# Four blocks of an output projection with another matmul stream: every second element, even then odd, backwards, and alternating PSUM banks

## Chip, cores and metric

The kernel runs on one core of one Trainium2 chip. The metric is the device time of one execution in microseconds (us); lower is better.

## What is computed

One decoder layer on 256 tokens of width 4096: a combined input projection, three head groups that run side by side (windowed attention with sinks and a relative bias, an mLSTM, cross-attention into 256 memory tokens), a SiLU gate on each, then one output projection and a LayerNorm over the scaled residual. The part that the change touches is the output projection:

```python
mix = jnp.concatenate([a_out, m_out, c_out], axis=-1).astype(x.dtype)
y = jnp.einsum("bse,ed->bsd", mix, w_out)
x = layer_norm(DEEPNORM_ALPHA * x.astype(jnp.float32) + y.astype(jnp.float32),
               ln_g, ln_b).astype(x.dtype)
```

Here `mix` is 256 x 4096 and `w_out` 4096 x 4096, all fp32.

## The kernel before, in words

Every large product keeps fp32 accuracy by splitting each operand into a rounded part and a rest, both of type fp32r: `split` (L91 to L93) makes `hi` with a cast on ScalarE (ACT) and `lo = raw - hi` on VectorE (DVE). A product is then three matmuls, hi by hi, hi by lo and lo by hi, which add into the same PSUM bank.

The kernel is one long list of blocks, written in program order; each engine executes its own instructions in that order. `fetch` (L141) keeps up to three weight tiles ahead: it issues the DMA of a 128 x 1024 weight tile into one of 4 `raw` buffers (L121, issued from SyncE) and the two splitting instructions into one of 3 `hi` and 3 `lo` buffers. `pump` (L160) after each tile lets small pieces of other work (attention, norms, evictions) into the instruction streams.

Two kinds of block use the weights. `cols_block` (L203) makes an output with features on partitions; its moving operand is the activations (512 columns for the `hi` weights, 256 for the `lo` weights). `rows_block` (L190) makes an output with tokens on partitions: the 128 x 128 piece of the activations is the stationary operand, and the weights are the moving operand, 512 columns at a time. It holds two PSUM banks, one for each half of the tokens (`rows0`, `rows1`). For each of 16 weight tiles, each of its two k-steps (`kk`) and each half of the tokens (`i`) it issues the three matmuls of `mm3` (L181 to L183): L181 has `mixh` stationary and `hi` moving, L182 `mixh` and `lo`, L183 `mixl` and `hi`. That is 16 x 2 x 2 x 3 = 192 matmuls of 512 columns in a block. A moving operand is `v[:, kk]`, 512 neighbouring fp32r elements in each partition.

The output projection is eight blocks of 512 output columns. Blocks 0 to 6 are one loop around `rows_block(mix_k, 512)` (L862); block 7 (`last0`, `last1`) is written out by hand. While block b + 1 runs, DVE adds the residual of block b (L806), takes its statistics (L807) and multiplies by the gain (L812); ACT and DVE also prepare rows of `ln_g` and `ln_b` (L788 to L791). LayerNorm itself follows after block 7.

The weights reach the device in a layout made on the host (`_layout`); the time of that is not part of the metric. Index 7 + b of `w_rows` holds block b of the output projection.

Of the kernel before, what the change touches and what calls it, by code (L numbers as in the profile page):

```python
# [16 lines left out]
P = 128  # L17
D = 4096
T = 256
KT = D // P  # L20
# [5 lines left out]
HELD = 8  # L26
WARM = 4
QS = 128 ** -0.5
XS = 256 ** -0.5


# [9 lines left out]
def hybrid_layer(ctx, tc, t, out):  # L41
# [3 lines left out]
    nc = tc.nc  # L45
# [95 lines left out]
    def fetch(look=LOOK):  # L141
        while stream and len(ready) <= look:
            item = stream.popleft()
            if item[0] == "act":
                load_act(*item[1:])
            elif item[0] == "first":
                load_first(*item[1:])
            else:
                ready.append(load_w(*item[1:]))
        return ready.popleft()  # L150

    def later(fn, gap=2):

        stages.append((fn, gap, clock[0]))

    def after(*fns):

        posts.extend((clock[0] + 1 + i, fn) for i, fn in enumerate(fns))

    def pump():  # L160
        clock[0] += 1
        due = [p for p in posts if p[0] <= clock[0]]
        posts[:] = [p for p in posts if p[0] > clock[0]]
        for _, fn in due:
            fn()
        while stages and clock[0] >= stages[0][1] + max(stages[0][2], clock[1]):
            clock[1] = clock[0]
            stages.popleft()[0]()
# [9 lines left out]
    def mm3(o, xhl, w, kk, tok, cols, first, last):  # L178
        xh, xl = xhl
        wh, wl = w[0][:, kk, cols], w[1][:, kk, cols]  # L180
        nc.tensor.matmul(o, xh[:, tok], wh, start=first, stop=False)  # L181
        nc.tensor.matmul(o, xh[:, tok], wl, start=False, stop=False)  # L182
        nc.tensor.matmul(o, xl[:, tok], wh, start=False, stop=last)  # L183

    tiles = [slice(0, P), slice(P, T)]

    def rows_tiles():
        return [acc.tile([P, 512], F32, name=f"rows{i}", tag="acc") for i in range(2)]

    def rows_block(get, ncol):  # L190


        ps = rows_tiles()
        for g in range(16):
            w = fetch()
            for kk in range(2):
                n = 2 * g + kk
                for i in range(2):
                    mm3(ps[i][:, :ncol], get(n), w, kk, tiles[i], slice(0, ncol), n == 0, n == KT - 1)
            pump()  # L200
        return ps
# [95 lines left out]
    for b in range(2):  # L297
        ps = rows_block(mem_k, 512)
        after(*[partial(split, *[v[:, b * 512:(b + 1) * 512] for v in memv[i]], ps[i]) for i in range(2)])
# [7 lines left out]
    def bias_of(b, heads, n):  # L307

        v = b[:, heads, :n]
        (part, rows, _) = v.ap  # L310
        return bass.AP(v.tensor, v.offset + n - 1, [part, rows, [-1, n]])
# [28 lines left out]
    def cross_head(h):  # L340
        p, pT = H("c_p"), [H(f"c_pT{v}", dt=F32R) for v in "hl"]

        def scores():
# [7 lines left out]
            nc.vector.tensor_reduce(nm, sc, axis=AX.X, op=ALU.max, negate=True)  # L351
            nc.vector.tensor_scalar_mul(nm, nm, XS)
            ssum = small.tile([P, 2], F32, name="c_sum")
            for i in range(2):
                nc.scalar.activation(p[:, i], sc[:, i], AF.Exp, bias=nm[:, i:i + 1], scale=XS,
                                     accum_out=ssum[:, i:i + 1])
# [45 lines left out]
    for b in range(3):  # L402
        after(partial(m_values, b, rows_block(x_k, 344)))
# [104 lines left out]
    def conv_of(j):  # L508
# [14 lines left out]
        def silu():  # L523
            if j < 4:
                nc.scalar.activation(mq[:, j], y[0], AF.Silu, bias=convb[:, j:j + 1])
            else:
                nc.scalar.activation(y[0], y[0], AF.Silu, bias=convb[:, j:j + 1])
                nc.vector.tensor_scalar_mul(mk[:, j - 4], y[0], QS)

# [60 lines left out]
    for b in range(2):  # L590
        ps = rows_block(x_k, 512)
        after(*[partial(m_out, b, i, ps) for i in range(2)])
# [58 lines left out]
    for b in range(2):  # L651
        ps = rows_block(x_k, 512)
# [9 lines left out]
    ps = rows_block(x_k, 512)  # L662
# [3 lines left out]
    def swa_group(g, aq, bias):  # L666
# [5 lines left out]
        def scores():  # L672
            ps = psum("a_s0", (P, 4, P))
            for h in range(4):
                nc.tensor.matmul(ps[:, h], aq[:, h, :P], ak[:, g, :P], start=True, stop=True)
            nc.vector.scalar_tensor_tensor(t0, ps, QS, bias_of(bias, slice(0, 4), P), op0=ALU.mult, op1=ALU.add)
            for hp in range(2):
                ps = psum("a_s1", (P, 2, 256))
                for j in range(2):
                    nc.tensor.matmul(ps[:, j], aq[:, 2 * hp + j, P:], ak[:, g], start=True, stop=True)  # L680
                nc.vector.scalar_tensor_tensor(t1[:, 2 * hp:2 * hp + 2], ps, QS,
                                               bias_of(bias, slice(2 * hp, 2 * hp + 2), 256), op0=ALU.mult, op1=ALU.add)
# [131 lines left out]
    def load_res(b):  # L814
        r = U(f"r{b}", (P, 2, 512))
        nc.sync.dma_start(r.rearrange("p a b -> p (a b)"), t["x_res"][b])
        res.append(r)
# [37 lines left out]
    for b in range(7):  # L855
        load_res(b)
        if b:
            later(partial(gain_rows, b - 1), 4)
        if b == 6:
            later(partial(gain_rows, 6), 4)  # L860
            later(partial(gain_rows, 7), 4)
        ps = rows_block(mix_k, 512)  # L862
        after(*[partial(fn, b, ps, i) for i in range(2) for fn in (residual, gain)])

    load_res(7)
# [4 lines left out]
    for g in range(16):  # L870
        w = fetch()
        for kk in range(2):
            n = 2 * g + kk
# [16 lines left out]
    for q in range(2):  # L890
        for g, w in held:
            for kk in range(2):
                n = 2 * g + kk
# [44 lines left out]
def _buckets():  # L938

    import numpy as np  # L940

    one = np.zeros((33, 384), np.float32)
    for u in range(384):
        dist = u - 127
        if not 0 <= dist < 128:
            one[32, u] = 1.0
            continue
        if dist < 16:
            b = dist
        else:  # L950
            b = 16 + int(np.float32(math.log(dist / 16.0)) / np.float32(math.log(8.0)) * np.float32(16))
        one[min(b, 31), u] = 1.0
    return one


def _layout(a):
    import numpy as np

    a = {k: np.asarray(v) for k, v in a.items()}
    w_in, w_kv, w_out = a["w_in"], a["w_mem_kv"], a["w_out"]  # L960

    def rows(w, width):

        n = w.shape[1] // width
        return w.reshape(16, 2, P, n, width).transpose(3, 0, 2, 1, 4).reshape(n, 16, P, 2 * width)

    def cols(w):

        n = w.shape[1] // P
        return w.reshape(4, 8, P, n, P).transpose(3, 0, 2, 1, 4).reshape(n, 4, P, 1024)  # L970

    wo = w_out.reshape(KT, P, D)[K_ORDER].reshape(D, D)
    xm = a["x"][0]
    d = {}
    d["w_rows"] = np.concatenate([
        rows(w_kv[:, 1024:], 512), rows(w_in[:, M_O:M_O + 1024], 512), rows(w_in[:, M_Z:M_Z + 1024], 512),
        rows(w_in[:, A_V:A_V + 512], 512), rows(wo, 512)])
    d["w_cols"] = np.concatenate([
        cols(w_kv[:, :1024]), cols(w_in[:, C_Q:C_Q + 1024]), cols(w_in[:, M_Q:M_Q + 1024]),
        cols(w_in[:, A_K:A_K + 512]), cols(w_in[:, A_Q:A_Q + 2048]), cols(w_in[:, C_Z:C_Z + 1024]),  # L980
        cols(w_in[:, A_Z:A_Z + 2048])])
    d["w_mv"] = rows(w_in[:, M_V:M_V + 1032], 344)
    for name, v in (("xT", xm), ("memT", a["mem"][0])):
        d[name] = v.T.reshape(KT, P, T).transpose(1, 0, 2).reshape(P, KT * T)
    d["x_res"] = xm.reshape(2, P, 8, 512).transpose(2, 1, 0, 3).reshape(8, P, 1024)
    d["conv_w"] = a["conv_w"].reshape(4, 8, P).transpose(2, 1, 0)
    d["conv_b"] = a["conv_b"].reshape(8, P).T
    d["b_i"], d["b_f"] = a["b_i"].reshape(4, 1), a["b_f"].reshape(4, 1)
    for name in ("m_norm_g", "rel_bias", "sinks", "ln_g", "ln_b"):
        d[name] = a[name]  # L990
    d["ident"] = np.eye(P, dtype=np.float32)
    d["causal"] = np.where(np.arange(P)[:, None] > np.arange(P)[None, :], np.float32(NEG), np.float32(0))
    d["sel"] = np.repeat(np.eye(4, dtype=np.float32)[:, :, None], P, axis=2)
    d["buckets"] = _buckets()
    d["neg"] = np.full((1, 16), NEG, np.float32)
    return {k: np.ascontiguousarray(v) for k, v in d.items()}
# [16 lines left out]
```

## Time and profile before

| | before |
|---|---|
| time, median of 2 runs | 1607.89 us (1607.05 to 1608.73) |
| profiled execution, its own time | 1607.13 us |
| span in the profile, first to last instruction | 1605.3 us |
| TensorE matmul (PE) busy | 1591.0 us, 99% of the span, 8298 matmuls |
| TensorE weight load (PEld) busy | 1358.9 us, 85% |
| VectorE (DVE) busy | 895.4 us, 56% |
| ScalarE (ACT) busy | 707.9 us, 44% |
| HBM traffic | 193 GB/s over the span |
| mean granted TensorE clock | 0.997 |

The profile is one execution, taken by the hardware profiler; its times are us unless marked ns. PE is TensorE's matmul stream, PEld its loads of stationary operands, which run beside the matmuls. The end of a matmul is modelled, and successive matmuls overlap, so the duration of one matmul is longer than the distance from its start to the next start. That distance, here called the step, is what the engine needs for each; it is read from starts. [...]

### The profile page before, as it was taken

How to read it: one execution, taken by the hardware profiler on the slowest of the kernel's cores; microseconds unless marked ns; L12 is line 12 of the kernel's file. 1: busy time of each engine (PE TensorE's matmuls, PEld its weight loads, DVE VectorE, ACT ScalarE, POOL GpSimd, SP SyncE). 2: the span in 40 equal slices, each digit the busy share in tenths (PEclk: the TensorE clock that was granted, in tenths of full speed). 3: DMA queues.
4: the chain of work that ended last, by engine and by line, in shares of the span. 5: the costliest groups of instructions: out<-in, count | busy, mean ns of one | idle time of the engine just before them, and what ended most of it. 6: DMA issues, size and time to landing. Idle time of an engine off the chain costs nothing.

```text
span 1605.3 us, 21127 instructions
## 1 busy us (share of the span) xinstructions
PE 1591.0 (99%) x8298; PEld 1358.9 (85%) x8298; DVE 895.4 (56%) x1120; ACT 707.9 (44%) x937; POOL 1.7 (0%) x20
## 2 busy tenths in 40 slices
PE   9999999999999999999999999999999999999997
PEld 6788888999888888888888888888888888888886
DVE  5555555545755457544466556555555555555656
ACT  5454444344643444444354445444444344444441
POOL 0000000000000000000000000000000000000000
PEclk9999999999999999999999999999999999999998
DMA  8667654566555555556645554555556765555553
GB/s 271 232 211 232 225 172 150 155 186 202 177 185 170 184 185 182 184 183 201 206 157 184 179 176 158 186 192 187 185 192 230 274 206 198 203 192 195 205 201 145
DMA packets 91355, 310.57 MB, mean 193 GB/s; under 512 B 10434, under 2 KB 13299, under 8 KB 91255
## 3 DMA queue, kind: packets, MB, share of 16 engines
q1 hardware_dynamic: 91254, 309.22, 57.9%
q8 instruction: 65, 1.06, 0.3%
q14 instruction: 36, 0.29, 0.0%
HBM read 304.96 MB, written 4.22 MB: 193 GB/s over the span
## 4 chain that ended last, share of the span: by engine, by line
PE 96%; DMA 2%; DVE 1%; ACT 1%; issue 0%; SPq 0%; DVEq 0%; ACTq 0%
PE cols L213 31%; PE cols L214 16%; PE rows L182 14%; PE rows L181 14%; PE rows L183 14%; DMA raw<-in_w_rows 1%; PE last L182 1%; PE last L183 1%; PE last L181 1%; ACT hi L92 0%; PE a_s L680 0%; DVE lo L93 0%; PE a_tp L714 0%; DMA raw<-in_w_cols 0%; DMA raw<-in_memT 0%; DVE r L849 0%
## 5 line engine op out<-in xcount | busy, mean ns | idle before, releaser
L93 DVE TENSOR_TENSOR lo<-raw,hi 128x1024 fp32r<-128x1024 f32 (+2 forms) x556 | 662.4, 1192 | 602.0 <-ACT hi L92 601.0
L92 ACT CAST hi<-raw 128x1024 fp32r<-128x1024 f32 (+2 forms) x556 | 568.4, 1023 | 746.3 <-PE rows L183 371.9
L213 PE MATMUL cols<-act,hi 128*128 128x512 f32 x2176 | 764.2, 394 | 0.0
L214 PE MATMUL cols<-act,lo 128*128 128x256 f32 x2176 | 610.6, 281 | 0.5 <-DVE lo L93 0.5
L213 PEld LDWEIGHTS cols<-act,hi 128*128 128x128 f32 x2176 | 409.2, 188 | 94.7 <-issue 0.9
L214 PEld LDWEIGHTS cols<-act,lo 128*128 128x128 f32 x2176 | 409.2, 188 | 1.3 <-DVE lo L93 0.9
L181 PE MATMUL rows<-hi,act 128*128 128x512 f32 (+1 forms) x640 | 241.5, 377 | 1.7 <-ACT hi L92 1.7
L182 PE MATMUL rows<-lo,act 128*128 128x512 f32 (+1 forms) x640 | 239.1, 374 | 1.0 <-DVE lo L93 1.0
L183 PE MATMUL rows<-hi,act 128*128 128x512 f32 (+1 forms) x640 | 238.1, 372 | 0.0
L182 PE MATMUL rows<-lo,mixh 128*128 128x512 f32 x448 | 176.9, 395 | 0.0
L181 PE MATMUL rows<-hi,mixh 128*128 128x512 f32 x448 | 176.8, 395 | 0.0
L183 PE MATMUL rows<-hi,mixl 128*128 128x512 f32 x448 | 176.6, 394 | 0.0
L181 PEld LDWEIGHTS rows<-hi,act 128*128 128x128 f32 x640 | 120.5, 188 | 23.2 <-ACT hi L92 2.7
L182 PEld LDWEIGHTS rows<-lo,act 128*128 128x128 f32 x640 | 120.6, 188 | 21.5 <-DVE lo L93 2.4
L183 PEld LDWEIGHTS rows<-hi,act 128*128 128x128 f32 x640 | 120.5, 188 | 19.8
L181 PEld LDWEIGHTS rows<-hi,mixh 128*128 128x128 f32 x448 | 84.2, 188 | 20.1
L183 PEld LDWEIGHTS rows<-hi,mixl 128*128 128x128 f32 x448 | 84.1, 188 | 20.1
L182 PEld LDWEIGHTS rows<-lo,mixh 128*128 128x128 f32 x448 | 84.1, 188 | 20.0
L92 ACT CAST mixh<-z 128x256 fp32r<-128x256 f32 x24 | 9.8, 406 | 40.2 <-DVE z L752 40.2
L219 ACT COPY low<-cols 128x256 f32<-128x256 f32 x68 | 25.0, 367 | 0.0
L93 DVE TENSOR_TENSOR act<-raw,act 128x512 fp32r<-128x512 f32 (+1 forms) x34 | 21.0, 655 | 6.4 <-ACT act L92 6.4
L92 ACT CAST act<-raw 128x512 fp32r<-128x512 f32 (+1 forms) x34 | 18.8, 593 | 9.9 <-DMA raw<-in_memT 6.2
(243 smaller groups left out, 653.2 us busy)
## 6 DMA issues: line engine op xcount, KB each, us to landing
raw<-in_w_cols SPq DMA_DIRECT2D x272, 512.0 KB, 3.3
raw<-in_w_rows SPq DMA_DIRECT2D x239, 512.0 KB, 3.3
raw<-in_w_mv SPq DMA_DIRECT2D x48, 344.0 KB, 3.2
raw<-in_xT SPq DMA_DIRECT2D x8, 512.0 KB, 4.5
r<-in_x_res SPq DMA_DIRECT2D x8, 512.0 KB, 4.6
out_y<-r SPq DMA_DIRECT2D x16, 256.0 KB, 2.1
raw<-in_memT SPq DMA_DIRECT2D x7, 512.0 KB, 5.0
bias<-bias_dram SPq DMA_DIRECT2D x4, 512.0 KB, 4.6
```

Of the source, the lines that this page charges most:

```text
L92: nc.scalar.copy(hi, raw)
L93: nc.vector.tensor_tensor(lo, raw, hi.bitcast(F32), op=ALU.subtract)
L181: nc.tensor.matmul(o, xh[:, tok], wh, start=first, stop=False)
L182: nc.tensor.matmul(o, xh[:, tok], wl, start=False, stop=False)
L183: nc.tensor.matmul(o, xl[:, tok], wh, start=False, stop=last)
L213: nc.tensor.matmul(ps, wh[:, kk], a, start=(k == 0), stop=False)
L214: nc.tensor.matmul(ps[:, 0], wl[:, kk], a[:, 0], start=False, stop=(k == KT - 1))
L219: nc.scalar.copy(low, ps[:, 1])
```

## The change

A table gives each of the eight blocks an order: block 1 "between", block 2 "evenodd", block 3 "backwards", block 4 "banks"; blocks 0, 5, 6 and 7 stay as they are. For a block with an order `rows_block` takes a new branch, which issues the same 192 matmuls of 512 columns from line 219 of the new kernel.

- between: step kk reads elements kk, kk + 2, kk + 4, ... of the 1024 in a partition, a step of two elements;
- evenodd: within its own 512 elements, the 256 even ones first and then the 256 odd ones, a step of two;
- backwards: its 512 elements from the last to the first, a step of minus one;
- banks: plain reading, but the six matmuls of a k-step are sorted so that successive ones go to `rows0` and `rows1` in turn, where before three went to `rows0` and then three to `rows1`.

The host permutes the columns of each weight tile of blocks 1 to 3, so that the product comes out the same. DMAs, casts, tile sizes and everything around the blocks are unchanged.

```diff
+ORDERS = ("", "between", "evenodd", "backwards", "banks", "", "", "")
...
-    def rows_block(get, ncol):
+    def moving(v, kk, order):
+        flat = v.rearrange("p a b -> p (a b)")
+        part = flat.ap[0]
+        if order == "between":
+            return flat[:, kk:1024:2]
+        if order == "backwards":
+            return bass.AP(v.tensor, flat.offset + kk * 512 + 511, [part, [-1, 512]])
+        if order == "evenodd":
+            return bass.AP(v.tensor, flat.offset + kk * 512, [part, [1, 2], [2, 256]])
+        return v[:, kk]
+
+    def rows_block(get, ncol, order=""):
...
+        if order:
+            for g in range(16):
+                w = fetch()
+                for kk in range(2):
+                    n = 2 * g + kk
+                    xh, xl = get(n)
+                    wh, wl = (moving(v, kk, order) for v in w)
+                    calls = [(i, a, b, j) for i in range(2) for j, (a, b) in enumerate(((xh, wh), (xh, wl), (xl, wh)))]
+                    if order == "banks":
+                        calls.sort(key=lambda c: (c[3], c[0]))
+                    for i, a, b, j in calls:
+                        nc.tensor.matmul(ps[i], a[:, tiles[i]], b, start=(n == 0 and j == 0),
+                                         stop=(n == KT - 1 and j == 2))
+                pump()
+            return ps
...
-        ps = rows_block(mix_k, 512)
+        ps = rows_block(mix_k, 512, ORDERS[b])
...
+    for b, order in enumerate(ORDERS):
+        w = d["w_rows"][7 + b].reshape(16, P, 2, 512)
+        if order == "between":
+            w = w.transpose(0, 1, 3, 2)
+        elif order == "backwards":
+            w = w[..., ::-1]
+        elif order == "evenodd":
+            w = w.reshape(16, P, 2, 2, 256).transpose(0, 1, 2, 4, 3)
+        d["w_rows"][7 + b] = w.reshape(16, P, 1024)
```

In blocks 1 to 3 no instruction changes its place on any engine. In block 4 the PE stream does. Its first k-step before, where `rows0` and `rows1` are the two PSUM banks, `hi` and `lo` the moving weights, and `mixh` and `mixl` the stationary activations:

```order
7234 L181 MATMUL rows0_11808<-hi_11770,mixh4_5405 128x512
7235 L182 MATMUL rows0_11808<-lo_11771,mixh4_5405 128x512
7236 L183 MATMUL rows0_11808<-hi_11770,mixl4_5406 128x512
7237 L181 MATMUL rows1_11809<-hi_11770,mixh4_5405 128x512
7238 L182 MATMUL rows1_11809<-lo_11771,mixh4_5405 128x512
7239 L183 MATMUL rows1_11809<-hi_11770,mixl4_5406 128x512
```

The same k-step of block 4 on PE in the changed kernel:

```order
7234 L219 MATMUL rows0_11808<-hi_11770,mixh4_5405 128x512
7235 L219 MATMUL rows1_11809<-hi_11770,mixh4_5405 128x512
7236 L219 MATMUL rows0_11808<-lo_11771,mixh4_5405 128x512
7237 L219 MATMUL rows1_11809<-lo_11771,mixh4_5405 128x512
7238 L219 MATMUL rows0_11808<-hi_11770,mixl4_5406 128x512
7239 L219 MATMUL rows1_11809<-hi_11770,mixl4_5406 128x512
```

The same six matmuls now change the bank at every step and not at every third; the `lo` tile is first read by the third matmul, not by the second.

## Rows read from the trace of the kernel before

**Rows 1.** The page, part 1: busy time, share of the span, instructions.

```profile
PE 1591.0 (99%) x8298; PEld 1358.9 (85%) x8298; DVE 895.4 (56%) x1120; ACT 707.9 (44%) x937; POOL 1.7 (0%) x20
```

**Rows 2.** The page, part 4: the chain that ended last, shares by engine.

```profile
PE 96%; DMA 2%; DVE 1%; ACT 1%; issue 0%; SPq 0%; DVEq 0%; ACTq 0%
```

**Rows 3.** Stretches of blocks 1 to 4: busy us (count) by engine, granted clock, DMA.

```profile
1274.70:1319.30 44.60, 44.60 (x193) 36.04 (x192) 25.08 (x26) 18.30 (x20) 0.00 (x0) 1.00 0.61 203
1319.30:1364.00 44.70, 44.70 (x193) 36.06 (x192) 25.07 (x26) 18.29 (x20) 0.00 (x0) 1.00 0.60 200
1364.00:1408.60 44.60, 44.60 (x193) 36.03 (x192) 25.07 (x26) 18.30 (x20) 0.00 (x0) 1.00 0.59 201
1408.60:1453.30 44.70, 44.70 (x193) 36.07 (x193) 25.07 (x26) 18.29 (x20) 0.00 (x0) 1.00 0.60 200
```

**Rows 4.** Who waited for whom in blocks 1 to 4 (total, times, longest).

```profile
ACT hi L92 <- PE rows L183: 106.7, 64, 1.8
DVE lo L93 <- ACT hi L92: 79.0, 61, 1.6
```

**Rows 5.** Chain in order of time, blocks 1 to 4: start, share on the chain, instruction.

```profile
1286.70 0.24 PE rows L181
...
1331.36 0.24 PE rows L181
...
1376.02 0.24 PE rows L181
...
1420.68 0.24 PE rows L181
...
1465.34 0.24 PE rows L181
```

**Rows 6.** PE in order of time, end of block 3, start of 4: start, duration.

```profile
1408.43 0.40 PE L183 MATMUL rows<-hi,mixl 128*128 128x512 f32 x1
1408.66 0.40 PE L181 MATMUL rows<-hi,mixh 128*128 128x512 f32 x1
1408.90 0.39 PE L182 MATMUL rows<-lo,mixh 128*128 128x512 f32 x1
1409.13 0.40 PE L183 MATMUL rows<-hi,mixl 128*128 128x512 f32 x1
1409.36 0.39 PE L181 MATMUL rows<-hi,mixh 128*128 128x512 f32 x1
1409.60 0.40 PE L182 MATMUL rows<-lo,mixh 128*128 128x512 f32 x1
1409.83 0.40 PE L183 MATMUL rows<-hi,mixl 128*128 128x512 f32 x1
1410.06 0.40 PE L181 MATMUL rows<-hi,mixh 128*128 128x512 f32 x1
```

**Rows 7.** PE in order of time, a stretch of 344-column fp32r matmuls.

```profile
301.08 0.32 PE L183 MATMUL rows<-hi,act 128*128 128x344 f32 x1
...
302.49 0.32 PE L183 MATMUL rows<-hi,act 128*128 128x344 f32 x1
```

**Rows 8.** Chain, eight passes of 256 columns in plain fp32 (attention scores).

```profile
809.67 1.73 PE a_s L680 x8
```

**Rows 9.** DVE in groups by form: bias read backwards (L681), all operands forwards (L806).

```profile
L681 DVE SCALAR_TENSOR_TENSOR t<-a_s,bias 128x512 f32<-128x512 f32 x8 | 5.5, 691 | 1.4 <-PE a_s L680 1.4
...
L806 DVE SCALAR_TENSOR_TENSOR r<-r,rows 128x512 f32<-128x512 f32 x8 | 5.4, 680 | 0.0
```

## Prediction

> **What bounds the kernel now.** I first read busy time by engine: PE is busy for 99% of the span, so only what TensorE does, or a wait that stops it, can move the end [rows 1]. The chain that ended last says the same: 96% of it is PE [rows 2]. Then I looked at the four blocks that the change touches. In each PE is busy for the whole stretch, the granted clock is 1.00, DVE has 25 of 44.6 us of work and ACT 18 us [rows 3]. The waits in these blocks are all on the supply side: ACT waits 64 times, 106.7 us together, for a matmul to free a buffer, and DVE waits for ACT [rows 4]. No wait of PE is listed. So weights arrive early, and a block lasts as long as its 192 matmuls. The chain gives that length five times over: from 1286.70 to 1331.36, 1376.02, 1420.68 and 1465.34, always 44.66 us [rows 5], which is 44.66 / 192 = 232.6 ns a matmul. The starts in the time order agree, 0.23 to 0.24 us apart [rows 6].
>
> The question is what sets these 232.6 ns. They come to 232.6 / 512 = 0.454 ns a column. Between the two rows with 344 columns lie nine steps in 1.41 us, 157 ns each, 0.456 ns a column [rows 7]. The price is therefore by the column, not by the instruction. [...]
>
> **The change part by part.** Nothing moves on ACT, DVE, POOL or SP, and in blocks 1 to 3 nothing moves on PE either; the counts and columns of matmuls are the same. Stationary operands keep their plain reading, and their loads take 36 of 44.6 us beside the matmuls [rows 3]. What changes is how the moving operand is read (576 matmuls) and which bank follows which (192).
>
> *Blocks 1 and 2, a step of two elements (384 matmuls).* The trace has no matmul with such a step, so I bound it. [...] No effect: 0. Upper end: if elements come in groups of neighbours and the delivery of groups is the limit, a step of two uses half of each group and needs twice the groups: 2 x 232.6 = 465.2 ns, +232.6 ns x 384 = +89.3 us. If instead the stream falls back to one element in two clocks, the pace of plain fp32, it takes 2 x 216.3 = 432.6 ns, +200.0 ns x 384 = +76.8 us. A stream with no margin should not survive losing half of each group, so I take the two slow values, and their middle, as nothing in the trace prefers one: 448.9 ns, +216.3 ns x 384 = +83.1 us.
>
> [...]
>
> *Block 3, backwards (192 matmuls).* Every neighbour is still used, in falling order. The nearest row is on another engine: DVE reads the attention bias backwards in 691 ns, where the same operation on as many elements, all forwards, takes 680 ns [rows 9], so there the direction costs nothing to speak of. The ends are 0 and the fallback of above, +200.0 to +232.6 ns x 192 = +38.4 to +44.7 us, if neighbours are only grouped in rising order. I take 0, by the DVE row, with less trust than that row deserves on its own engine.
>
> *Block 4, alternating banks (192 matmuls).* Before, each third step changes the bank (L183 to L181) and the others stay. In [rows 6] the changes are 1408.43 to 1408.66, 1409.13 to 1409.36 and 1409.83 to 1410.06, 0.23 us each; the steps within a bank are 0.23 to 0.24. So neither staying nor changing has a price larger than the rounding of 0.01 us; over 192 matmuls that bounds it at -2 to +2 us. [...] I take 0. `lo` is wanted one step later, which only helps; the last matmul into `rows0` lies one step nearer the end, and DVE's residual is issued a whole weight tile later.
>
> *What is covered, and what is late next.* A slower block gives the supply more time: its chain already waits for PE [rows 4], and DMA is at 60% [rows 3]. PE's own stream is the cover of everything else, so a cost on it shows in full; blocks 5 to 7 cannot win it back, since they run without waits already. The residual work of a slower block lies beside longer blocks.
>
> **Sum.** +83.1 + 0 + 0 = +83.1 us on the profiled execution's own time of 1607.13 us (a span of 1605.3 and 1.8 around it): 1690.2 us. The median of the runs is 1607.89, 0.8 us above that execution; that is far inside the bounds of the terms.
>
> **The rivals.**
>
> First, not slower: the delivery has margin for half-used groups. [...] It decides if a block with a step of two stays under 46 us. [...]
>
> Second, all three orders fall back: only a step of plus one is grouped. Then 576 matmuls pay 200.0 to 232.6 ns, +115 to +134 us, 1722 to 1741 us. For it: a grouping for rising neighbours is the simplest. Against it: the backward reading on DVE is free, though at a lower rate of elements.
>
> Third, the step of two is free and only the falling order pays: +38 to +45 us, 1646 to 1652 us. It needs a rule of direction without a rule of step; nothing in the profile speaks for it.
>
> **How the numbers follow.** Forecast, steps of two pay and the rest is free: 0.54, with 1684 to 1697 us as its own range. No change: 0.25. All three pay: 0.15. Only backwards: 0.04. Anything else (a fall of the granted clock in a slow stretch, a worse penalty): 0.02. The first rival and the forecast hold most of the chance together, so the range reaches from the first rival to the forecast's upper end: 1604 to 1698 us, which leaves out the case of all three and the odd ones, about 0.17 to 0.2. Two per cent, 32 us, is about what a measurement of this kernel can tell from no change. Faster by more is out of reach: lifting the whole shortfall in all four blocks gives 768 x 16.3 ns = 12.5 us; I leave 0.01 for what I have not seen. Within: 0.26, the first rival and a little. Slower: 0.73, the other cases together.
>
> **What would show it.** In the changed kernel's profile all four blocks have line 219. Right: blocks 1 and 2 last 83 to 89 us each (192 x 432.6 to 465.2 ns), blocks 3 and 4 44.7 us, with starts 0.23 us apart; PE stays without waits, the granted clock stays at 1.00, and ACT's wait for PE in blocks 1 and 2 grows by the added time. Wrong: a block with a step of two at 44.7 us (first rival), block 3 as long as they (second), block 4 other than 44.7 by over 2 us, or a granted clock below 1.00 in the slow stretch, which would make part of the cost the clock's and not the reading's.

## The result, and the profile after

The changed kernel takes 1690.59 us (median of 2 runs, 1690.35 to 1690.83) against 1607.89 before: a ratio of 1.051, 95% interval 1.047 to 1.056. The forecast was 1690 us. Its profiled execution has a span of 1688.6 us, 83.3 us longer than before.

The stretches of blocks 1 to 4 answer to [rows 3]; the columns are the same (stretch, then busy us and count for PE, PEld, DVE, ACT and POOL, granted clock, DMA share, GB/s):

```profile
1273.60:1360.40 86.80, 86.80 (x193) 39.80 (x192) 25.08 (x26) 18.24 (x20) 0.00 (x0) 1.00 0.33 111
1360.40:1447.30 86.90, 86.90 (x194) 39.85 (x193) 25.07 (x26) 18.24 (x20) 0.00 (x0) 1.00 0.31 103
1447.30:1492.10 44.80, 44.80 (x194) 36.07 (x193) 25.08 (x26) 18.28 (x20) 0.00 (x0) 1.00 0.55 188
1492.10:1536.70 44.60, 44.60 (x194) 36.04 (x193) 25.07 (x26) 18.31 (x20) 0.00 (x0) 1.00 0.59 200
```

Each stretch is one block of 192 matmuls (the count takes in the ones that lap over its ends). The two blocks with a step of two last 86.8 us, 452 ns a matmul; the backward block 44.8 us, 233 ns; the one with alternating banks 44.6 us, 232 ns. The granted clock stays at 1.00, and DVE and ACT have the same work as before in all four. The supply idles, as the DMA column shows: 103 to 111 GB/s in the slow blocks against 200.

The chain of work that ended last, over the same four blocks (start, length, what):

```profile
1273.76 263.07 PE rows L219 x768
```

Not one of the 768 matmuls waits for another engine: 263.07 us in one piece. Before, four blocks took 4 x 44.66 = 178.6 us [rows 5]. The 84.4 us between are the whole change; the span grew by 1.1 us less because the blocks began 1.1 us sooner in this execution (block 1 at 1273.60 us, in [rows 3] at 1274.70).

The starts on PE at the beginning of block 2 (start, duration) answer to [rows 6]:

```profile
1360.43 0.63 PE L219 MATMUL rows<-hi,mixh 128*128 128x512 f32 x1
1360.89 0.63 PE L219 MATMUL rows<-lo,mixh 128*128 128x512 f32 x1
1361.34 0.63 PE L219 MATMUL rows<-hi,mixl 128*128 128x512 f32 x1
1361.79 0.63 PE L219 MATMUL rows<-hi,mixh 128*128 128x512 f32 x1
```

0.45 us from start to start, where it was 0.23. The waits in these blocks answer to [rows 4] (waiter, releaser, total us, times, longest):

```profile
ACT hi L94 <- PE rows L219: 189.7, 64, 4.4
...
PEld rows L219 <- issue: 94.0, 384, 0.3
```

ACT waits for PE as often as before, 64 times, and 83.0 us longer in total: the added time turns up as idle time of the supply. The 384 waits of PEld, 0.3 us at most, are as many as the two slow blocks have matmuls. The trace shows no releaser for them, and they delay nothing, since PE runs without a gap.

### The profile page after: what moved, and what is told of

Read it like the earlier page. It is cut to its first block, busy times and chain, and to the rows that moved or that the text cites. A ratio compares the mean times of both kernels' runs of the same rounds, so it can differ in the third digit from the quotient of the medians.

```text
span 1688.6 us, 21127 instructions
## 1 busy us (share of the span) xinstructions
PE 1675.1 (99%) x8298; PEld 1366.2 (81%) x8298; DVE 895.4 (53%) x1120; ACT 708.0 (42%) x937; POOL 1.7 (0%) x20
## 4 chain that ended last, share of the span: by engine, by line
PE 97%; DMA 1%; DVE 1%; ACT 0%; issue 0%; SPq 0%; DVEq 0%; ACTq 0%
PE cols L242 29%; PE rows L219 16%; PE cols L243 15%; PE rows L184 11%; PE rows L183 11%; PE rows L185 10%; DMA raw<-in_w_rows 1%; PE last L184 1%; PE last L185 1%; PE last L183 1%; PE a_s L709 0%; PE a_tp L743 0%; DMA raw<-in_w_cols 0%; ACT hi L94 0%; DVE r L878 0%; DVE lo L95 0%
## 5 line engine op out<-in xcount | busy, mean ns | idle before, releaser
L219 PE MATMUL rows<-hi,mixl 128*128 128x512 f32 x256 | 126.3, 513 | 0.0
L219 PE MATMUL rows<-hi,mixh 128*128 128x512 f32 x256 | 126.2, 513 | 0.0
L219 PE MATMUL rows<-lo,mixh 128*128 128x512 f32 x256 | 126.2, 513 | 0.0
L219 PEld LDWEIGHTS rows<-hi,mixh 128*128 128x128 f32 x256 | 50.6, 198 | 37.1 <-issue 31.3
L219 PEld LDWEIGHTS rows<-lo,mixh 128*128 128x128 f32 x256 | 50.5, 197 | 37.1 <-issue 31.4
L219 PEld LDWEIGHTS rows<-hi,mixl 128*128 128x128 f32 x256 | 50.6, 198 | 37.1 <-issue 31.4
L184 PE MATMUL rows<-lo,mixh 128*128 128x512 f32 x192 | 75.8, 395 | 0.0
L183 PE MATMUL rows<-hi,mixh 128*128 128x512 f32 x192 | 75.7, 394 | 0.0
L185 PE MATMUL rows<-hi,mixl 128*128 128x512 f32 x192 | 75.7, 394 | 0.0
```

The lines of the kernel that those rows point to most:

```text
L219: nc.tensor.matmul(ps[i], a[:, tiles[i]], b, start=(n == 0 and j == 0), stop=(n == KT - 1 and j == 2))
```

## The experiments

The time came out as forecast, but two accounts of it stood on record: groups of neighbours that are half used (465 ns), and a fall to the pace of plain fp32 (433 ns). 452 ns lies between them, and both would say the same of many other orders. So the experiments give each block of one kernel its own reading order and read the length of each block from the trace. The runs on the changed kernel put a table of orders in the place of its three named orders:

```diff
+        if order in PATTERNS:
+            per, off, dims = PATTERNS[order]
+            return bass.AP(v.tensor, flat.offset + kk * per + off, [part, *[list(d) for d in dims]])
         return v[:, kk]
```

`per` is the distance between the first elements of the two k-steps, `off` the element at which the first of them begins. `dims` are (step, count) pairs from the outermost to the innermost, over the 1024 elements of a partition; the host permutes the columns to match wherever the order is a permutation.

**Steps and groups.**

```diff
+ORDERS = ('', 'four', 'eight', 'three', 'back2', 'mixed4', 'pairs', '')
+PATTERNS = {
+    'four': (512, 0, [(1, 4), (4, 128)]),
+    'eight': (512, 0, [(1, 8), (8, 64)]),
+    'three': (256, 0, [(1, 2), (3, 256)]),
+    'back2': (512, 510, [(1, 2), (-2, 256)]),
+    'mixed4': (512, 0, [(4, 128), (1, 2), (2, 2)]),
+    'pairs': (2, 0, [(4, 256), (1, 2)]),
+}
```

> Seven blocks, each its own reading of the 512 moving elements: block 0 plain, 1 step of four, 2 step of eight, 3 step of three, 4 step of minus two, 5 each group of four neighbours as 0, 2, 1, 3, 6 pairs of neighbours with a step of four between pairs. Block 3 reads elements of other columns, so its part of the output is not the product. Measured so far: 232.6 ns a matmul plain, 452 ns at a step of two. Theory A (groups of four neighbours, one group every 1.76 ns, is what the stream can be given): step of four and of eight about 905 ns, step of three (384 groups) about 677 ns, minus two and pairs 452 ns, 0-2-1-3 233 ns, since each group is visited once; 905 or 452 there if a group is not kept. Rival B (any step but plus or minus one falls back to one element in two clocks): 452 ns for steps of three, four, eight and minus two and for 0-2-1-3, 233 ns for pairs. Rival C (groups of two neighbours): 452 ns for all steps and for 0-2-1-3, 233 ns for pairs. Time by A: 1608 + 192 x (672 + 672 + 444 + 219 + 0 + 219 ns) = about 2035 us; by B and C about 1608 + 5 x 42 = 1819 us.

The time was 1817.8 us. The stretches of blocks 1 to 6 (columns as above):

```profile
1273.30:1361.80 88.50, 88.50 (x194) 39.92 (x193) 25.06 (x26) 18.24 (x20) 0.00 (x0) 1.00 0.34 109
1361.80:1444.60 82.80, 82.80 (x193) 39.45 (x192) 25.07 (x26) 18.24 (x20) 0.00 (x0) 1.00 0.32 107
1444.70:1532.20 87.50, 87.50 (x194) 39.80 (x193) 25.06 (x26) 18.27 (x20) 0.00 (x0) 1.00 0.32 103
1532.20:1621.80 89.60, 89.60 (x194) 40.32 (x193) 25.06 (x26) 18.25 (x20) 0.00 (x0) 1.00 0.30 100
1621.80:1666.50 44.70, 44.70 (x194) 36.09 (x193) 25.07 (x26) 18.31 (x20) 0.00 (x0) 1.00 0.56 189
1666.50:1752.80 86.30, 86.30 (x192) 39.56 (x191) 28.42 (x34) 21.27 (x28) 0.00 (x0) 1.00 0.32 108
```

Theory A, groups of four for one stream, falls: a step of four takes 461 ns (88.5 / 192), not 905, a step of eight 432 ns (82.9 / 192, from its start to the next), and a step of three 456 ns, not 677. It is right on 0, 2, 1, 3 and on the pairs, and there B and C are both wrong: 0, 2, 1, 3 within a group is free at 233 ns, where both had 452, and pairs of neighbours cost 452 ns, where both had 233. The total, 1817.8 us against 1819 by B and C, agrees by luck: their two misses cancel. None of the three accounts is right.

**Repeated, shifted and crossed readings.**

```diff
+ORDERS = ('split', 'same', 'same4', 'odd', 'swap', 'halves', 'two4', '')
+PATTERNS = {
+    'split': (512, 0, [(256, 2), (1, 256)]),
+    'same': (512, 0, [(0, 512)]),
+    'same4': (512, 0, [(0, 128), (1, 4)]),
+    'odd': (256, 1, [(1, 512)]),
+    'swap': (512, 1, [(2, 256), (-1, 2)]),
+    'halves': (512, 0, [(1, 256), (256, 2)]),
+    'two4': (512, 0, [(8, 64), (1, 4), (4, 2)]),
+}
```

> Seven blocks again: block 0 plain in two dimensions, 1 the same element 512 times, 2 the same four neighbours 128 times, 3 plain but starting one element later, 4 neighbours swapped in pairs (1, 0, 3, 2), 5 the two halves of 512 in turn (0, 256, 1, 257), 6 two groups of four in turn (0, 4, 1, 5, ...). Blocks 1, 2 and 3 read other data than the product needs, so their part of the output is not the product. [...] Theory A (groups of four): start one later 233 ns, swapped 233 ns; halves in turn visit 512 groups, 905 ns if only one group is at hand; two groups in turn 905 ns likewise, 233 ns if two are at hand. Rival B (step): 233 ns for the start, 452 ns for halves and two groups. Rival C (pairs): start one later above 233 ns if pairs are aligned, swapped 233 ns, halves and two groups 452 ns.

The time was 1595.45 us, less than before, in a single run. Blocks 1 to 6:

```profile
1274.80:1316.30 41.50, 41.50 (x194) 36.30 (x192) 25.07 (x26) 18.23 (x20) 0.00 (x0) 1.00 0.71 218
1316.30:1357.80 41.50, 41.50 (x193) 36.33 (x192) 25.07 (x26) 18.24 (x20) 0.00 (x0) 1.00 0.66 217
1357.80:1403.30 45.50, 45.50 (x193) 36.29 (x193) 25.07 (x26) 18.32 (x20) 0.00 (x0) 1.00 0.59 197
1403.30:1448.00 44.70, 44.70 (x194) 36.08 (x193) 25.07 (x26) 18.31 (x20) 0.00 (x0) 1.00 0.60 200
1448.00:1489.40 41.40, 41.40 (x193) 36.26 (x192) 25.07 (x26) 18.28 (x20) 0.00 (x0) 1.00 0.67 215
1489.40:1530.60 41.20, 41.20 (x192) 36.09 (x191) 28.24 (x34) 21.27 (x28) 0.00 (x0) 1.00 0.66 216
```

Two readings stand out. With the same element, or the same four, over and over, a matmul takes 216.1 ns (41.5 / 192). If the 232.6 ns of the plain order were the pace of the fp32r arithmetic, these blocks would take them as well; so the 16.5 ns between are a shortage of delivery, which is gone when nothing new is fetched. And the two orders that every account had called slow or at best neutral, the two halves in turn and two groups of four in turn, also run at 216 ns (41.4 / 192), though they read every element once: they are 7% faster than the plain order. Two more change little: 237 ns for a start one element later, 233 ns for neighbours swapped.

That forms theory D, an account inferred from these times. By it the elements at even places of the reading order and those at odd places are served as two streams; each takes at best an element in 0.845 ns, as plain fp32 does in [rows 8] (1.73 us for 8 x 256 columns), and each pays for visiting another group of four neighbours. By this account both streams use two elements of each group in the plain order (232.6 ns); in the crossed orders (0, 4, 1, 5, ...) each uses all four (216 ns), and with a step of two each uses one (452 ns).

**Plain fp32, where there would be one stream.** Blocks 1 to 4 use plain fp32 matmuls in place of fp32r on the same data, two passes of 512 columns each. Block 1 reads plainly, block 2 with a step of two (the even elements, then the odd), block 3 with a step of four, and block 4 the same element 512 times (its part of the output is not the product).

```diff
                     for i, a, b, j in calls:
+                        a, b = a.bitcast(F32), b.bitcast(F32)
```

> [...] Block 1 should take 192 x 865 ns = 166 us. Theory A (a group of four every 1.76 ns): a step of two needs 256 groups a pass, 450 ns against 433 ns, so 166 to 174 us; a step of four needs 512 groups, 900 ns a pass, about 345 us; the same element 166 us. [...] Rival C (groups of two): 450 ns a pass for steps of two and four, about 174 us.

Blocks 1 to 4 (384 passes each):

```profile
1274.30:1439.10 164.80, 164.80 (x386) 72.96 (x385) 25.07 (x26) 18.23 (x20) 0.00 (x0) 1.00 0.19 58
1439.10:1611.90 172.80, 172.80 (x386) 72.15 (x385) 25.07 (x26) 18.25 (x20) 0.00 (x0) 1.00 0.17 52
1611.90:1957.40 345.50, 345.50 (x385) 79.84 (x384) 25.07 (x26) 18.24 (x20) 0.00 (x0) 1.00 0.08 26
1957.40:2122.20 164.80, 164.80 (x384) 72.41 (x383) 25.07 (x26) 18.23 (x20) 0.00 (x0) 1.00 0.17 54
```

These times fit groups of four and a single stream. Plain reading and the same element take 429 ns a pass, a step of two 450 ns, a step of four 900 ns (345.5 / 384), each as theory A had it. The step of four decides: C had 450 there, as for the step of two, and by B, where a step costs no more than the pace of plain fp32, all four blocks would be alike. By the account of A this is 900 / 512 = 1.757 ns for each element that needs a group of its own, and 450 / 256 = 1.758 ns for each two that share one. In the changed kernel each of D's two streams needs 256 groups a matmul: 256 x 1.757 = 449.8 ns, against 452 measured, with a price taken from another data type and another order. For the plain fp32r order the same price does less well: 128 groups for each stream come to 128 x 1.757 = 224.9 ns, between the 216 ns without new groups and the 232.6 measured. D thus gives the direction of the plain order's 16.5 ns and about half of their size (224.9 less 216.1).

**The change without its steps of two.**

```diff
-ORDERS = ("", "between", "evenodd", "backwards", "banks", "", "", "")
+ORDERS = ('', '', '', 'backwards', 'banks', '', '', '')
```

> The change without its steps of two: block 3 backwards and block 4 alternating banks alone. If the whole loss lies in the steps of two, the time is that of before, 1607.9 us, within 0.3 us (backwards read 233.5 ns, banks 232.2 ns a matmul in the changed kernel: +0.2 and -0.1 us). If backwards or banks pay something that the other two hide, the time is over 1610 us.

1607.3 us (median of 10 runs) against 1607.49 for the kernel before, ratio 0.9998 (0.9989 to 1.0008). Backwards and alternating banks are free within the noise, and the loss is in the steps of two alone.

**Orders that tell two streams from clashes of near reads.**

```diff
+ORDERS = ('', 'half4', 'quarters', 'sixteen', 'eight', 'two4', 'halves', '')
+PATTERNS = {
+    'half4': (1, 0, [(8, 128), (2, 2), (4, 2)]),
+    'quarters': (512, 0, [(1, 128), (128, 4)]),
+    'sixteen': (512, 0, [(1, 16), (16, 32)]),
...
+}
```

> Seven fp32r blocks: 1 every second element in the order 0, 4, 2, 6, 8, 12, 10, 14 (then the odd ones by the other k-step), 2 the four quarters in turn (0, 128, 256, 384, 1, ...), 3 a step of sixteen, 4 a step of eight, 5 two groups of four in turn, 6 the two halves in turn. All are permutations of the product's columns. Theory D: the elements at even places of the reading order and those at odd places are served as two streams, each at most one element in two clocks, and each pays 1.76 ns for every visit to a new group of four neighbours. Then block 1 takes 233 ns a matmul though it has a step of two (each stream uses two of each group it visits); the quarters take 452 ns if a stream keeps one group, 216 ns if it keeps two; steps of sixteen and eight 432 to 452 ns; two groups and halves in turn 216 ns again. Rival F (neighbouring reads clash when they fall in the same part of the memory, and reads far apart do not): the quarters 216 ns, block 1 at 216 ns or below 233 ns, a step of sixteen below 432 ns. A step of two as such (theory B) says 452 ns for block 1.

Blocks 1 to 3:

```profile
1273.60:1317.80 44.20, 44.20 (x193) 36.03 (x192) 25.06 (x26) 18.25 (x20) 0.00 (x0) 1.00 0.63 207
1317.80:1371.70 53.90, 53.90 (x194) 36.74 (x193) 25.06 (x26) 18.27 (x20) 0.00 (x0) 1.00 0.51 166
1371.70:1454.90 83.20, 83.20 (x194) 39.54 (x193) 25.06 (x26) 18.25 (x20) 0.00 (x0) 1.00 0.34 114
```

Block 1 reads with a step of two, like the change, but in the order 0, 4, 2, 6, so that each stream uses two of every group: 230 ns instead of 452. A step of two is thus not slow in itself. This does not decide between D and the clashing rival F, though: D had 233 ns, F anything below 233. The quarters in turn miss: 281 ns, where D had 452 or 216 and F 216. By D each stream there goes to and fro between two groups, and this costs less than a new group and more than staying. A step of sixteen takes 433 ns, within the expectation of 432 to 452. The steps of eight (432 ns), two groups in turn and halves in turn (216 ns) repeat what the runs above had shown.

**The same orders in plain fp32.** With the `bitcast` line of the other fp32 run:

```diff
+ORDERS = ('', 'halves', 'two4', 'mixed4', 'pairs', '', '', '')
```

> Blocks 1 to 4 with plain fp32 matmuls in place of fp32r (two passes of 512 columns each): block 1 the two halves in turn, 2 two groups of four in turn, 3 each group as 0, 2, 1, 3, 4 pairs with a step of four. Theory D with a single stream for plain fp32: every read of blocks 1 and 2 visits another group, 512 x 1.757 = 900 ns a pass, 345 us a block, so the two orders that are best for fp32r are the worst here; block 3 visits each group once, 430 ns, 165 us; block 4 visits 256 groups, 450 ns, 173 us. Rival F (clashes of near reads): blocks 1 and 2 not above 430 ns, 165 us.

```profile
1274.20:1481.70 207.50, 207.50 (x386) 73.03 (x385) 25.07 (x26) 18.24 (x20) 0.00 (x0) 1.00 0.15 47
1481.70:1690.20 208.50, 208.50 (x386) 73.17 (x385) 25.07 (x26) 18.24 (x20) 0.00 (x0) 1.00 0.13 43
1690.20:1855.00 164.80, 164.80 (x386) 72.98 (x385) 25.07 (x26) 18.23 (x20) 0.00 (x0) 1.00 0.17 54
1855.00:2027.30 172.30, 172.30 (x385) 71.92 (x384) 25.06 (x26) 18.24 (x20) 0.00 (x0) 1.00 0.17 52
```

The direction is D's and against the rival of clashes, which had 430 ns at most: the orders that are best for fp32r are slow in fp32, 540 and 543 ns a pass, while order within a group (429 ns) and pairs (449 ns) come out as D said. The size is not: 540 ns, not 900. Going to and fro between two groups costs 540 / 512 = 1.055 ns an element, less than the 1.757 ns measured with a new group for each element. The quarters above come near this if D's two streams share them: half as many elements for each, 540 / 2 = 270 ns, against 281 measured.

**A version that uses it, first for the blocks with weights as moving operand.** From the kernel before:

```diff
+    def crossed(v):
+        return v.rearrange("p (a c b) -> p a b c", c=2, b=4)
...
-        wh, wl = w[0][:, kk, cols], w[1][:, kk, cols]
+        wh, wl = crossed(w[0][:, kk, cols]), crossed(w[1][:, kk, cols])
...
-        return w.reshape(16, 2, P, n, width).transpose(3, 0, 2, 1, 4).reshape(n, 16, P, 2 * width)
+        w = w.reshape(16, 2, P, n, width).transpose(3, 0, 2, 1, 4)
+        return w.reshape(n, 16, P, 2, width // 8, 4, 2).swapaxes(5, 6).reshape(n, 16, P, 2 * width)
```

> From the kernel before: every block with tokens on partitions, the last one too, reads its weights as two groups of four in turn (0, 4, 1, 5, 2, 6, 3, 7), with the columns permuted on the host so that the product stays as it was. Theory D: 215.8 in place of 232.6 ns for 512 columns, about 145.8 in place of 156.5 ns for 344, and about 109 in place of 118 ns for 256: 2784 x 16.8 + 576 x 10.7 + 192 x 9 ns = 54.7 us, less about 6 us in the first two blocks, where PE waits for the weights: about 1559 us, between 1553 and 1566. If the gain in one block only shifts a wait into the next, the time stays above 1590 us.

1554.69 us against 1606.59 for the kernel before, ratio 0.968 (0.966 to 0.970). Block 1 of the projection in its profile:

```profile
1244.00:1285.40 41.40, 41.40 (x193) 36.27 (x192) 25.07 (x26) 18.25 (x20) 0.00 (x0) 1.00 0.70 229
```

**Then for all blocks.** In addition:

```diff
-                nc.tensor.matmul(ps, wh[:, kk], a, start=(k == 0), stop=False)
-                nc.tensor.matmul(ps[:, 0], wl[:, kk], a[:, 0], start=False, stop=(k == KT - 1))
+                nc.tensor.matmul(ps, wh[:, kk], crossed(a.rearrange("p a b -> p (a b)")), start=(k == 0), stop=False)
+                nc.tensor.matmul(ps[:, 0], wl[:, kk], crossed(a[:, 0]), start=False, stop=(k == KT - 1))
...
-            nc.scalar.copy(low, ps[:, 1])
-            nc.vector.tensor_tensor(out(), ps[:, 0], low, op=ALU.add)
+            hi, lo = (ps[:, n].rearrange("p (a b c) -> p a c b", b=4, c=2) for n in range(2))
+            nat = [v.rearrange("p (a c b) -> p a c b", c=2, b=4) for v in (low, out())]
+            nc.scalar.copy(nat[0], lo)
+            nc.vector.tensor_tensor(nat[1], hi, nat[0], op=ALU.add)
```

> As f0_rows_crossed, and the blocks with features on partitions read their activations as two groups of four in turn as well; the eviction puts the tokens back in order with strided reads of PSUM on ScalarE and VectorE. Theory D: 2176 x (16.8 + 9) ns = 56 us more, about 1503 us, between 1495 and 1515, if the evictions stay off the path; if the supply of weights (DMA, ScalarE, VectorE) cannot follow the faster stream, up to 1540 us.

1506.74 us against 1606.59, ratio 0.939 (0.937 to 0.940): 100 us faster than before. The page, part 1, and PE in order of time in a block with features on partitions:

```profile
PE 1489.3 (99%) x8298; PEld 1344.1 (89%) x8298; DVE 894.4 (59%) x1120; ACT 706.0 (47%) x937; POOL 1.7 (0%) x20
```

```profile
929.77 0.38 PE L216 MATMUL cols<-act,hi 128*128 128x512 f32 x1
929.99 0.27 PE L217 MATMUL cols<-act,lo 128*128 128x256 f32 x1
...
931.08 0.38 PE L216 MATMUL cols<-act,hi 128*128 128x512 f32 x1
```

The same 8298 matmuls keep PE busy for 1489.3 us, against 1591.0 [rows 1]. Four pairs of 512 and 256 columns take 1.31 us, 328 ns a pair; the expectation had 325, and 3 ns x 2176 pairs are most of the 8 us between the 48 us that this step brought (1554.69 less 1506.74) and the 56 us expected. The evictions stay off the path: none of the waits that the profile lists for PE names their copy or their sum, and the longest of them, 3.5 us, lies in LayerNorm (waiter, releaser, total us, times, longest):

```profile
PE row_ps L841 <- DVE col L836: 3.5, 1, 3.5
```

ScalarE's copy out of PSUM takes as long as before, strided (L224 here) or not (L219 in the kernel before):

```profile
L219 ACT COPY low<-cols 128x256 f32<-128x256 f32 x68 | 25.0, 367 | 0.0
L224 ACT COPY low<-cols 128x256 f32<-128x256 f32 x68 | 25.1, 369 | 0.0
```

## Why the prediction was right

**What bounds the kernel.** Confirmed: PE alone. The whole loss stands on PE, without a wait, and the supply idled for as long (ACT's waits grew by 83.0 us).

**A stream with no margin.** This carried the forecast as the author's estimate, since the trace of before shows PE with no other order of reading, and it was right: with nothing new to fetch the same matmul takes 216.1 ns (41.5 / 192) and not 232.6, and with a step of two 452. What it left out is how delivery is organised. It thought of one stream with groups of neighbours; the times of the runs fit two streams, each with groups of four.

The sum has a term of one element in two clocks. No run shows how many clocks an element takes. What [rows 8] shows is the pace of plain fp32, 1.73 us / 8 = 216.3 ns for 256 columns, and the 432.6 ns are twice that; 512 columns in plain fp32 then took 429 ns, and the steps of two in fp32r 452 ns. The clocks in theories B and D are the same estimate.

**The term for the steps of two.** 448.9 ns was the middle of two accounts, and 452.2 ns (86.83 / 192) was measured: +84.3 us for the two blocks against +83.1. The sum was right, but neither account was. "Twice the groups" fails at a step of four, which costs 461 ns and not 4 x 232.6 = 930; the fall to the pace of plain fp32 fails at 230 ns for a step of two in crossed order, and at 900 ns for plain fp32 with a step of four. Two streams with 1.757 ns a group give 450 ns. What is left of "twice the groups" is that by theory D each stream visits 256 groups instead of 128; the price came out lower than the 232.6 / 128 = 1.817 ns a group that the prediction's 465.2 ns implied. The middle was a hedge that fell near the truth by luck, not a derivation of it.

**Backwards and banks.** Both were set at 0. Measured 44.8 and 44.6 us a block against 44.66, and 0.9998 as a ratio when they stand alone. By theory D each stream still uses two of each group when read backwards, so the free result needs no trust in the DVE row [rows 9].

**The rivals.** The first rival, a delivery with margin for half-used groups, is refuted: the same matmul takes 216, 233 or 452 ns by the order alone, and the change's steps of two are the slowest of these. Plain fp32 nearly has such a margin: two of each four cost 450 ns against 429, 5% more, and one of four costs 900. For fp32r theory D counts the elements within each of its two streams: the plain order has two for each group (232.6 ns), the crossed order four (216 ns), a step of two one (452 ns). The second and third rivals fall with block 3 (44.8 us).

**The upper limit on a gain.** The prediction gave 16.3 ns a matmul as the most that could be lifted. No run that it had showed this term: it is 232.6 ns less the 216.3 ns of 256 columns in plain fp32 [rows 8], taken by estimate as the least for 512 columns in fp32r. The size was right (17.0 ns in the crossed orders, 232.6 less 41.4 / 192); that an order of reading lifts it was missed, and so was that it applies to the fp32r matmuls of all weight blocks, where it is worth 100 us.

## What to carry to other kernels

When an fp32r stream on TensorE runs without waits and its price goes by the column (here 0.454 ns at 512 columns and 0.456 at 344), try the order of its moving operand early: reading two groups of four in turn (0, 4, 1, 5, 2, 6, 3, 7) gave 7% a matmul (216 against 233 ns) and 6% of the kernel's time here (1506.74 against 1606.59 us), with only an access pattern and a permuted layout. Do not carry that order to plain fp32, where it cost a quarter more (543 against 429 ns). And let one kernel carry several variants, one for each of its equal blocks, when the trace can time each block by itself: one run then does the work of six.

## What was not expected

- An order that jumps 1 KB or 16 bytes at each element is faster for fp32r than reading straight on: 216 against 233 ns for 512 columns.
- Going to and fro between two groups costs 1.055 ns an element in plain fp32, a new group for each element 1.757 ns. Why a return is cheaper is open.
- Among the orders with one element of each group for a stream the times spread: 432 ns (step of eight), 433 (sixteen), 452 (two, and pairs), 456 (three), 461 (four), 467 (minus two). The two-stream account gives 450 for all; the spread was not followed up. The steps of eight and sixteen lie at the pace that the prediction took from plain fp32 (432.6 ns), below what D's price allows. The 237 ns of a plain reading that starts one element later were not followed up either.
- That the streams are the even and the odd places of the reading order is inferred from how the orders fall out; no view of the profile shows the streams themselves. One rival stands untested: two successive elements fetched together as a pair, which pays for a new group only if the pair before it did not have that group. By counting, it needs new groups in as many pairs as each stream of D has visits, in every fp32r order tried here.
